# Loading the residual's row tiles one by one between the first stores of a two-layer hybrid encoder

## The chip, the cores and the metric

The kernel runs on one core of a Trainium2 chip. The metric is the device time of one execution in microseconds (us), the median over runs. The core's engines are TensorE (PE in the profile, its weight loads PEld), VectorE (DVE), ScalarE (ACT), GpSimd (POOL) and SyncE (SP), which here issues all transfers. Sixteen DMA engines move the data.

## The reference, cut to what matters

Two encoder layers on 1024 tokens of 1024 channels, in float32. Layer 0 mixes tokens by attention, layer 1 by pooling; each then attends into 256 memory tokens and applies a gated MLP. Before each of these parts stands an RMS norm with a factor (gain) per channel, behind it the residual is added.

```python
def rmsnorm(x, gain):
    x32 = x.astype(jnp.float32)
    y = x32 * lax.rsqrt(jnp.mean(x32 * x32, axis=-1, keepdims=True) + EPS)
    return (y * gain.astype(jnp.float32)).astype(x.dtype)

for i in range(DEPTH):
    if i % N_MIXERS == 0:
        x = x + axial_gqa_attention(rmsnorm(x, attn_norm[ia]), attn_w_qkv[ia],
                                    attn_q_gain[ia], attn_k_gain[ia], attn_w_o[ia])
    ...
    x = x + memory_cross_attention(rmsnorm(x, xattn_norm[i]), rmsnorm(mem, mem_norm[i]),
                                   xattn_w_q[i], xattn_w_kv[i], xattn_w_o[i])
    x = x + conv_gated_ffn(rmsnorm(x, ffn_norm[i]), ffn_w_up[i], ffn_conv_w[i],
                           ffn_conv_b[i], ffn_w_down[i])
return rmsnorm(x, final_norm)
```

The change lies where layer 0's attention ends: `o @ w_o`, the residual, and the norm ahead of the cross-attention.

## The kernel before, in words

The tokens stand in eight row tiles X0 to X7 of 128 tokens x 1024 channels in SBUF, 512 KB each. A product is made as three products of split operands (a high and a low part; lines 746 to 748), accumulated in a PSUM bank. The large products of the cross-attention's query projection are made with seven block products where eight would be usual (class `Seven`): for this the normalised tiles are transposed on TensorE (`turn`, L323) and halves of them are added and subtracted.

`Kernel.run` is the program. `attention` gives the head outputs OT. `load_rows` loads one half (512 columns) of `attn_w_o` in four pieces of 512 KB into the staging buffers `scr` (six of them, shared by all stages) and splits them. Then run loads the tiles X0 to X7 of the input x (L2128) in the order 0, 2, second half of the weights, 4, 6, 1, 3, 5, 7. `cross` follows; its first act is to load the channel factors `xattn_norm` into an `scr` buffer, one copy for each of the 128 partitions (`bcast`, L712, 512 KB), and to make `Seven` with them.

`rows_by` gives three functions for one product of a row tile t with a half n of the weights: `gemm` (24 matmuls into one bank), `add` (the bank onto X[t], L1556), `freed` (gives buffers back). `Seven.begin` runs them in an order written out by hand, 16 steps (n, t): (0,0) (0,2) (1,0) (1,2) (0,4) (1,4) (0,6) (1,6) (0,1) (1,1) (0,3) (1,3) (0,5) (0,7) (1,5) (1,7). Each step does in this order: `gemm`; `free` (here `freed`); at seven of the steps a `turn` of a tile that is done, the first (tile 0) in step (1,2); `add`; `save`, a 256 KB store of the half X[t] to the DRAM tensor Xq (L314), which is read back later as the residual; and, with both halves there, the tile's sum of squares on ScalarE (L727), the root on GpSimd (L719, L721) and `norm` (L318), which overwrites the tile with its normalised values on VectorE. So `norm` needs the factors, the root, and both stores of that tile landed.

All transfers are issued by SP in program order; where SP has to wait for one, all behind it wait. Their completion is counted on eight counters, DMAHW0 to DMAHW7, that are used in turn; a transfer whose counter still has one under way is held until that one, eight places ahead, has landed.

Of the kernel before, what the change touches and what calls it, by code (L numbers as in the profile page):

```python
# [16 lines left out]
P = 128  # L17
# [280 lines left out]
class Seven:  # L298
# [71 lines left out]
    def load(self, f, j):  # L370

        c = self.columns(f)[j]
        src = self.w[:, c:c + P].rearrange("(k p) n -> p k n", p=P)
        self.nc.sync.dma_start(out=self.raws[f][j].rearrange("p (k n) -> p k n", k=NK), in_=src)
# [254 lines left out]
class Kernel:  # L629
# [590 lines left out]

        return (self.R.hv(h).rearrange("p (k n) -> p k n", k=4)[:, k % 4, cols] for h in hs[k // 4 * 2:k // 4 * 2 + 2])

    def cross(self, i, X, steps=None, mixer=None, over={}):

        nc, R, a = self.nc, self.R, self.a
        Xd = self.tc.dram_tile([S, D], F32, name=f"Xq{i}")
        U = Seven(self, a["xattn_w_q"][i], lambda f: (2 * f * P, (2 * f + 1) * P), X, Xd, self.bcast(a["xattn_norm"][i]))
        plan_sums = self.down_sums(i)  # L1230
        q, nf, mem, kT, v, sm, PT, O, wo = {}, D // (2 * P), {}, [], [], {}, {}, {}, {}
        both = lambda t: [(f"X{t}", j) for j in range(2)]
# [6 lines left out]
        def plan_split(plan, name, f, late):  # L1239
# [3 lines left out]
            def high():  # L1243
                hs = q[c] = R.get_halves(1)
                nc.scalar.activation(R.hv(hs[0]), U.bank[f][name], AF.Copy, scale=XHD ** -0.5)

            def low():
                h, l = (R.hv(x) for x in q[c])
                nc.vector.scalar_tensor_tensor(l, U.bank[f].pop(name), XHD ** -0.5, h.bitcast(F32), op0=OP.mult, op1=OP.subtract)
            ins = [(u, 0), (u, 1)]  # L1250
# [184 lines left out]
        def main():  # L1435
            order = U.order(nf)
            if steps:
                U.begin(*steps, lambda: None)
                U.H["T4"] = [R.get(), R.get()]
                over.update({"DVE": 6.5, "ACT": 4.9})  # L1440
            plan = Plan(R, over, {"scr": 2 if steps else 6, "A": 2, "B": 4, "half": len(R.freed)})
            if mixer:
                mixer(plan, U, X)
                order[:4] = [(2, 0), 3, (1, 0), 5, (2, 1), None]
# [673 lines left out]
    def run(self):  # L2118
        nc, R, a = self.nc, self.R, self.a
        OT = self.attention()  # L2120
        ws = [self.load_rows(a["attn_w_o"][0], 0)]
        xp = self.ctx.enter_context(self.tc.tile_pool(name="xres", bufs=1, reuse_waits="tile"))
        X = [xp.tile([P, D], F32, name=f"X{t}") for t in range(NT)]
        for t in (0, 2, None, 4, 6, 1, 3, 5, 7):
            if t is None:
                ws.append(self.load_rows(a["attn_w_o"][0], 1))
            else:
                nc.sync.dma_start(out=X[t], in_=a["x"][0][t * P:(t + 1) * P, :])  # L2128

        def lhs(t, k):  # L2130
            return (R.v(s, 8)[:, k, t % 4 // 2 * P:(t % 4 // 2 + 1) * P] for s in OT[t // 4 * 2 + t % 2])

        def free(t):
            if t % 4 >= 2:
                R.put(*OT[t // 4 * 2 + t % 2])

        steps = self.rows_by(lhs, X, free, lambda n, k: self.blk(ws[n], k, slice(0, 512)), lambda n: R.put(*ws[n]))
        lhs, *ops = self.cross(0, X, steps)
        ready = []
        gemm, add, over = self.ffn(0, lhs, X, *ops, lambda plan: ready.extend([self.pool_weights(plan)]))  # L2140
        lhs, *ops = self.cross(1, X, None, partial(self.pool_mixer, gemm, add, ready[0]), over)
        self.ffn(1, lhs, X, *ops, out=self.out[0])


# [30 lines left out]
```

## Time and profile before

| | us |
|---|---|
| median of 3 runs | 2509.69 (2505.69 to 2514.07) |
| the profiled execution | 2508.51 |
| its span, first to last instruction | 2506.7 |
| TensorE busy in it | 2473.4 |
| VectorE busy in it | 1958.6 |
| ScalarE busy in it | 1348.4 |
| GpSimd busy in it | 436.2 |

The profile shows that one execution; all times within it are microseconds from the start of the span. A row of a timeline has start, length, engine, line, operation, output<-inputs and shapes, and in brackets the idle time ahead of it with what ended it. A row of waits names the waiting engine and line, what it waited for, the total, the number of times and the longest. The granted TensorE clock was 0.998 of full speed over the span. The stage of this change stands between 528 and 634 us.

### The profile page before, as it was taken

How to read it: one execution, taken by the hardware profiler on the slowest of the kernel's cores; microseconds unless marked ns; L12 is line 12 of the kernel's file. 1: busy time of each engine (PE TensorE's matmuls, PEld its weight loads, DVE VectorE, ACT ScalarE, POOL GpSimd, SP SyncE). 2: the span in 40 equal slices, each digit the busy share in tenths (PEclk: the TensorE clock that was granted, in tenths of full speed). 3: DMA queues.
4: the chain of work that ended last, by engine and by line, in shares of the span. 5: the costliest groups of instructions: out<-in, count | busy, mean ns of one | idle time of the engine just before them, and what ended most of it. 6: DMA issues, size and time to landing. Idle time of an engine off the chain costs nothing.

```text
span 2506.7 us, 37225 instructions
## 1 busy us (share of the span) xinstructions
PE 2473.4 (99%) x13435; PEld 2129.7 (85%) x13435; DVE 1958.6 (78%) x2899; ACT 1348.4 (54%) x2307; POOL 436.2 (17%) x594
## 2 busy tenths in 40 slices
PE   9999999999999999999999999999999999999998
PEld 8999999978898888888888888889888888887887
DVE  7779989864986379888889776987559888888875
ACT  6558888852655255555555334655335555554542
POOL 5756666631011000000000003102010000000001
PEclk9999999999999999999999999999999999999999
DMA  7100000042595124243258553388223324337852
GB/s 253 43 2 14 13 14 13 13 171 68 187 317 183 57 79 126 84 122 110 85 170 285 198 182 111 126 283 306 73 72 109 114 84 124 108 93 255 278 189 97
DMA packets 314733, 326.50 MB, mean 130 GB/s; under 512 B 14133, under 2 KB 248861, under 8 KB 314549
## 3 DMA queue, kind: packets, MB, share of 16 engines
q1 hardware_dynamic: 314549, 324.12, 39.9%
q8 instruction: 106, 1.74, 0.3%
q14 instruction: 78, 0.64, 0.1%
HBM read 232.48 MB, written 82.58 MB: 126 GB/s over the span
## 4 chain that ended last, share of the span: by engine, by line
PE 87%; issue 4%; DVE 3%; DMA 2%; ACT 2%; POOL 1%; SPq 0%; POOLq 0%; DVEq 0%; ACTq 0%
PE pB L746 21%; PE pB L748 21%; PE pB L747 21%; PE pA L779 4%; PE pB L740 4%; PE pA L748 3%; PE pA L746 3%; PE pA L747 3%; PE pB L1193 2%; PE pB L1192 2%; DVE R L668 1%; PE pB L323 1%; ACT R L665 1%; DMA scr<-in_ffn_w_down 1%; PE pA L2058 1%
## 5 line engine op out<-in xcount | busy, mean ns | idle before, releaser
L746 PE MATMUL pB<-R,R 128*128 128x512 f32 (+1 forms) x2764 | 1024.3, 371 | 8.4 <-DVE scr L439 3.3
L748 PE MATMUL pB<-R,R 128*128 128x512 f32 (+1 forms) x2760 | 1016.4, 368 | 1.3 <-DVE R L668 1.2
L747 PE MATMUL pB<-R,R 128*128 128x512 f32 (+1 forms) x2764 | 1017.3, 368 | 0.0
L746 PEld LDWEIGHTS pB<-R,R 128*128 128x128 f32 x2764 | 521.1, 189 | 100.7 <-DVE scr L439 4.6
L748 PEld LDWEIGHTS pB<-R,R 128*128 128x128 f32 x2760 | 520.1, 188 | 89.0 <-DVE R L668 2.6
L747 PEld LDWEIGHTS pB<-R,R 128*128 128x128 f32 x2764 | 521.2, 189 | 85.6 <-DVE R L674 0.4
L665 ACT ACTIVATE R<-scr 128x512 fp32r<-128x512 f32 (+2 forms) x340 | 256.9, 781 | 218.3 <-DMA scr<-Gs 60.3
L668 DVE TENSOR_TENSOR R<-scr,R 128x512 fp32r<-128x512 f32 (+2 forms) x340 | 291.6, 887 | 21.5 <-ACT R L665 20.9
L668 DVE TENSOR_TENSOR R<-X,R 128x512 fp32r<-128x512 f32 x374 | 252.5, 686 | 67.5 <-ACT R L665 66.6
L665 ACT ACTIVATE R<-X 128x512 fp32r<-128x512 f32 x374 | 231.7, 630 | 135.8 <-PE pB L747 65.4
L719 POOL TENSOR_SCALAR ms<-ss 128x1 f32<-128x1 f32 (+1 forms) x53 | 14.9, 281 | 1659.0 <-ACT R L727 1280.7
L437 ACT COPY scr<-pB 128x512 f32<-128x512 f32 x156 | 91.3, 585 | 188.3 <-PE pB L748 182.5
L673 ACT ACTIVATE PT<-pB 128x512 fp32r<-128x512 f32 x256 | 140.1, 604 | 56.0 <-PE pB L740 55.7
L789 DVE TENSOR_REDUCE nm<-pA 128x1 f32<-128x1024 f32 x125 | 152.5, 1220 | 20.5 <-PE pA L779 20.5
L674 DVE TENSOR_TENSOR PT<-pB,PT 128x512 fp32r<-128x512 f32 x256 | 163.5, 679 | 5.0 <-ACT PT L673 4.9
L1765 DVE TENSOR_TENSOR X<-pB,X 128x512 f32<-128x512 f32 (+1 forms) x145 | 99.3, 686 | 85.5 <-PE pB L748 84.5
L795 POOL TENSOR_SCALAR scr<-scr,inv 128x1024 f32<-128x1024 f32 x125 | 140.7, 1127 | 70.1 <-DVE inv L794 69.8
L746 PE MATMUL pA<-R,R 128*128 128x512 f32 (+1 forms) x420 | 150.6, 359 | 0.0
L748 PE MATMUL pA<-R,R 128*128 128x512 f32 (+1 forms) x420 | 150.2, 358 | 0.2 <-DVE R L668 0.2
L747 PE MATMUL pA<-R,R 128*128 128x512 f32 (+1 forms) x420 | 150.0, 357 | 0.0
L779 PE MATMUL pA<-R,R 128*128 128x512 f32 x512 | 145.4, 405 | 0.0
L792 ACT ACTIVATE scr<-pA,nm 128x1024 f32<-128x1024 f32 x125 | 139.8, 1118 | 1.5 <-DVE nm L789 0.5
(172 smaller groups left out, 3485.0 us busy)
## 6 DMA issues: line engine op xcount, KB each, us to landing
X<-in_ffn_w_up SPq DMA_DIRECT2D x82, 512.0 KB
Gs<-X SPq DMA_DIRECT2D x105, 256.0 KB
scr<-in_ffn_w_down SPq DMA_DIRECT2D x45, 512.0 KB
scr<-Gs SPq DMA_DIRECT2D x35, 512.0 KB
scr<-in_xattn_w_kv SPq DMA_DIRECT2D x32, 512.0 KB
scr<-Gs SPq DMA_DIRECT2D x42, 384.0 KB
Wt<-scr SPq DMA_DIRECT2D x44, 256.0 KB
Gs<-scr SPq DMA_DIRECT2D x42, 256.0 KB
```

Of the source, the lines that this page charges most:

```text
L665: self.nc.scalar.activation(hi, src, AF.Copy)
L668: self.nc.vector.tensor_tensor(out=lo, in0=src, in1=hi.bitcast(F32), op=OP.subtract)
L673: nc.scalar.activation(hi, src, AF.Copy)
L674: nc.vector.tensor_tensor(out=lo, in0=src, in1=hi.bitcast(F32), op=OP.subtract)
L740: self.nc.tensor.transpose(p[:, k, :], src[:, b * P:(b + 1) * P], self.ident)
L746: mm(out, ah, bh, start=start, stop=False)
L747: mm(out, ah, bl, start=False, stop=False)
L748: mm(out, al, bh, start=False, stop=stop)
L779: nc.tensor.matmul(s[:, kh * 512:(kh + 1) * 512], q, R.v(K[part][kh], 4)[:, kv], start=part == 0, stop=part == 1)
L789: nc.vector.tensor_reduce(nm, s, axis=AX.X, op=OP.max, negate=True)
L792: nc.scalar.activation(pr, s, AF.Exp, bias=nm, accum_out=rs)
L795: nc.gpsimd.tensor_scalar(pr, pr, ri, 1.0, op0=OP.mult, op1=OP.mult)
```

## The change

`run` loads only tiles 0, 2 and 4 ahead of the residual, and the channel factors between the weights' second half and tile 4. The tiles 6, 1, 3, 5 and 7 are loaded one by one from a function `between` that takes the place of `freed` in the steps: in step (1,2) tile 6, in (0,4) tile 1, in (1,4) tile 3, in (1,6) tile 5, in (0,1) tile 7. `between` runs ahead of its step's `add` and `save`, so on SP's queue each load stands directly behind the store of the step before. `cross` gets the factors as an argument; for layer 1 they are loaded at the call, which is the same place on the queue.

```diff
-    def cross(self, i, X, steps=None, mixer=None, over={}):
+    def cross(self, i, X, gain, steps=None, mixer=None, over={}):
...
-        U = Seven(self, a["xattn_w_q"][i], lambda f: (2 * f * P, (2 * f + 1) * P), X, Xd, self.bcast(a["xattn_norm"][i]))
+        U = Seven(self, a["xattn_w_q"][i], lambda f: (2 * f * P, (2 * f + 1) * P), X, Xd, gain)
...
-        for t in (0, 2, None, 4, 6, 1, 3, 5, 7):
-            if t is None:
-                ws.append(self.load_rows(a["attn_w_o"][0], 1))
-            else:
-                nc.sync.dma_start(out=X[t], in_=a["x"][0][t * P:(t + 1) * P, :])
+
+        def load(t):
+            nc.sync.dma_start(out=X[t], in_=a["x"][0][t * P:(t + 1) * P, :])
+        load(0)
+        load(2)
+        ws.append(self.load_rows(a["attn_w_o"][0], 1))
+        gain = self.bcast(a["xattn_norm"][0])
+        load(4)
+        later = {(1, 2): 6, (0, 4): 1, (1, 4): 3, (1, 6): 5, (0, 1): 7}
...
-        steps = self.rows_by(lhs, X, free, lambda n, k: self.blk(ws[n], k, slice(0, 512)), lambda n: R.put(*ws[n]))
-        lhs, *ops = self.cross(0, X, steps)
+        gemm, add, freed = self.rows_by(lhs, X, free, lambda n, k: self.blk(ws[n], k, slice(0, 512)), lambda n: R.put(*ws[n]))
+
+        def between(n, t):
+            freed(n, t)
+            if (n, t) in later:
+                load(later[n, t])
+        steps = gemm, add, between
+        lhs, *ops = self.cross(0, X, gain, steps)
...
-        lhs, *ops = self.cross(1, X, None, partial(self.pool_mixer, gemm, add, ready[0]), over)
+        lhs, *ops = self.cross(1, X, self.bcast(a["xattn_norm"][1]), None, partial(self.pool_mixer, gemm, add, ready[0]), over)
```

SP's queue from behind the weights' second half on, before: X0_ to X7_ are the row tiles, scr_ is the buffer of the factors, Xq0_ the tensor that the stores write; in brackets what SP waits for.

```order
L2128 DMA X4_7408<-in_x 128x1024 [waits DMAHW1_49,PE_49]
L2128 DMA X6_7410<-in_x 128x1024 [waits DMAHW2_49,PE_49]
L2128 DMA X1_7405<-in_x 128x1024 [waits DMAHW3_49]
L2128 DMA X3_7407<-in_x 128x1024 [waits DMAHW4_49]
L2128 DMA X5_7409<-in_x 128x1024 [waits DMAHW5_49]
L2128 DMA X7_7411<-in_x 128x1024 [waits DMAHW6_49]
L712 DMA scr_7439<-in_xattn_norm 128x1024 [waits DMAHW7_49,Pool_49]
L314 DMA Xq0_7438<-X0_7404 128x512 [waits DMAHW0_49,DVE_49]
L314 DMA Xq0_7438<-X2_7406 128x512 [waits DMAHW1_49,DVE_49]
L314 DMA Xq0_7438<-X0_7404 128x512 [waits DMAHW2_49,DVE_49]
L314 DMA Xq0_7438<-X2_7406 128x512 [waits DMAHW3_49,DVE_49]
```

The same place of the changed kernel:

```order
L712 DMA scr_7430<-in_xattn_norm 128x1024 [waits DMAHW2_49,DMAHW1_49,Pool_49]
L2126 DMA X4_7408<-in_x 128x1024 [waits PE_49]
L314 DMA Xq0_7435<-X0_7404 128x512 [waits DMAHW5_49,DMAHW3_49,DVE_49]
L314 DMA Xq0_7435<-X2_7406 128x512 [waits DMAHW6_49,DMAHW4_49,DVE_49]
L314 DMA Xq0_7435<-X0_7404 128x512 [waits DVE_49]
L2126 DMA X6_7410<-in_x 128x1024 [waits PE_49]
L314 DMA Xq0_7435<-X2_7406 128x512 [waits DMAHW7_49,DVE_49]
L2126 DMA X1_7405<-in_x 128x1024 [waits DMAHW0_49]
L314 DMA Xq0_7435<-X4_7408 128x512 [waits DMAHW2_49,DMAHW1_49,DVE_49]
L2126 DMA X3_7407<-in_x 128x1024
```

Five loads have gone from ahead of tile 0's second store, the third of the stores, to places behind it, and the factors stand ahead of tile 4.

VectorE at the first two norms, before:

```order
L1556 TENSOR_TENSOR X0_7404<-pB_7507,X0_7404 128x512 [waits PE_49]
L318 SCALAR_TENSOR_TENSOR X0_7404<-X0_7404,rs_7539,scr_7439 128x1024 [waits DMAHW2_49,DMAHW0_49,DMAHW7_49,Activation_49,Pool_49]
L1556 TENSOR_TENSOR X2_7406<-pB_7542,X2_7406 128x512 [waits PE_49]
L318 SCALAR_TENSOR_TENSOR X2_7406<-X2_7406,rs_7584,scr_7439 128x1024 [waits DMAHW1_49,DMAHW3_49,Activation_49,Pool_49]
L674 TENSOR_TENSOR R3_70<-pB_7567,R2_69 128x4x128 [waits PE_49,Activation_49]
L674 TENSOR_TENSOR R5_72<-pB_7568,R4_71 128x4x128 [waits PE_49,Activation_49]
L1556 TENSOR_TENSOR X4_7408<-pB_7593,X4_7408 128x512 [waits PE_49]
```

And of the changed kernel:

```order
L1556 TENSOR_TENSOR X0_7404<-pB_7502,X0_7404 128x512 [waits PE_49]
L318 SCALAR_TENSOR_TENSOR X0_7404<-X0_7404,rs_7534,scr_7430 128x1024 [waits DMAHW3_49,DMAHW1_49,DMAHW5_49,Activation_49,Pool_49]
L1556 TENSOR_TENSOR X2_7406<-pB_7537,X2_7406 128x512 [waits PE_49]
L318 SCALAR_TENSOR_TENSOR X2_7406<-X2_7406,rs_7580,scr_7430 128x1024 [waits DMAHW4_49,DMAHW7_49,Activation_49,Pool_49]
L674 TENSOR_TENSOR R3_70<-pB_7563,R2_69 128x4x128 [waits PE_49,Activation_49]
L674 TENSOR_TENSOR R5_72<-pB_7564,R4_71 128x4x128 [waits PE_49,Activation_49]
L1556 TENSOR_TENSOR X4_7408<-pB_7589,X4_7408 128x512 [waits DMAHW2_49,PE_49]
```

No instruction of VectorE has moved. The norm waits for the same transfers under other counters (the factors and the tile's two stores), and the first add of tile 4, as those of tiles 6, 1, 3, 5 and 7, now waits for its load by a counter of its own. TensorE, ScalarE and GpSimd issue the same instructions in the same order.

## Prediction

> **What bounds the kernel now.** I read the page first (busy shares and the chain), then TensorE's waits over the whole run, then the chain, the stretches and the timelines around the one long wait.
>
> ```profile
> span 2506.7 us, 37225 instructions
> ...
> PE 2473.4 (99%) x13435; PEld 2129.7 (85%) x13435; DVE 1958.6 (78%) x2899; ACT 1348.4 (54%) x2307; POOL 436.2 (17%) x594
> ...
> PE 87%; issue 4%; DVE 3%; DMA 2%; ACT 2%; POOL 1%; SPq 0%; POOLq 0%; DVEq 0%; ACTq 0%
> ```
>
> TensorE is busy 99% of the span, and the chain that ends last runs over it. A change that moves only transfers can win only where TensorE now stands still. Its waits, longest in total first (us, times, longest):
>
> ```profile
> PE pB L323 <- DVE X L318: 3.9, 2, 3.5
> PE pB L746 <- DVE scr L439: 3.3, 6, 1.0
> PE pB L740 <- POOL scr L795: 3.0, 5, 1.0
> ```
>
> The longest single one, 3.5 us, is a transpose (L323, `turn`) waiting for the normalisation of a row tile (L318, `norm`). The others are at most 1.0 us each, at places that the change doesn't touch. The chain through the long one (start, length, what):
>
> ```profile
> 545.75 0.70 DVE X L1556
> ...
> 546.47 6.66 DMA Xq<-X
> ...
> 553.35 1.29 DVE X L318
> ...
> 554.69 1.09 PE pB L323 x8
> ```
>
> This is step (1,0) of the residual: the second half of tile 0 is added (L1556) and stored (Xq<-X), and `norm` may overwrite the tile only when the store has landed, 6.66 us after its issue. VectorE's waits in the stretch 515 to 660 us show what is usual:
>
> ```profile
> DVE X L318 <- POOL rs L721: 13.6, 6, 2.6
> DVE X L318 <- DMA Xq<-X: 6.9, 1, 6.9
> ```
>
> Six norms waited at most 2.6 us, for GpSimd's root (L721), and one waited 6.9 us, for the store. Why that store is slow is told by the stretches (last two columns: share of the DMA engines' time, GB/s) and by SP's queue:
>
> ```profile
> 540.00:546.00 6.00, 6.00 (x29) 4.95 (x27) 3.40 (x4) 2.12 (x2) 0.00 (x0) 1.00 1.03 419
> 546.00:551.00 5.00, 5.00 (x23) 3.94 (x21) 0.44 (x1) 1.15 (x2) 0.75 (x2) 1.00 0.97 375
> 551.00:555.00 4.00, 0.46 (x4) 0.32 (x4) 1.65 (x2) 0.00 (x0) 0.00 (x0) 1.00 0.05 19
> 555.00:561.00 6.00, 6.00 (x32) 5.05 (x30) 2.72 (x4) 3.10 (x6) 0.76 (x2) 1.00 0.11 44
> ```
> ```profile
> 533.51 5.56 SPq L2128 DMA_DIRECT2D X<-in_x  x6
> 540.07 0.33 SPq L712 DMA_DIRECT2D scr<-in_xattn_norm  x1
> ...
> 542.86 0.33 SPq L314 DMA_DIRECT2D Xq<-X  x1
> ...
> SPq L314 <- DMA X<-in_x: 1.9, 2, 1.0
> ```
>
> Until 551 the DMA engines are full, then almost idle: the store was issued behind six tile loads and the factors. SP's last row times the loads: a transfer waits for the one eight places ahead (the counters in the order's rows above), so the store at 542.86 went out when tile 4 had landed (about 542.8, after 1.0 us of waiting), and the next store waited the other 0.9 us, from about 543.2 to 544.1, for tile 6. That is 1.25 us for a 512 KB load in a full queue (419 GB/s).
>
> **The change part by part.** It adds and removes no instruction of TensorE, VectorE, ScalarE or GpSimd. SP issues the same eight loads, one factor row and stores in another order.
>
> *Five loads leave the queue ahead of the store.* Before, from the landing of tile 6 at 544.1: four tiles and the factors, 5 x 1.25 = 6.25 us, two stores of half the size, 2 x 0.63, and the store itself, 0.63, give 552.2 by this count. The stretches have the engines full to 551 and the chain has the landing at 553.13 (546.47 + 6.66), so 1 to 2 us lie between the last byte and the signal. Now only the factors and tile 4 follow the last weight piece:
>
> ```profile
> 541.42 1.06 ACT L673 ACTIVATE R<-scr 128x1024 fp32r<-128x1024 f32 x1 [0.33 <-DMA scr<-in_attn_w_o]
> ...
> 533.68 0.75 POOL L1206 TENSOR_TENSOR R<-scr,R 128x256 fp32r<-128x256 f32 x1
> ```
>
> The piece has landed at 541.4; plus 2 x 1.25 and two stores, 2 x 0.63, that is 545.2. The store issued at 546.47 finds an empty queue. The factors now wait for GpSimd's L1206, whose buffer they take, until 534.43, and tile 4 behind them leaves about 1 us later than now; both still stand behind that piece, so this costs nothing.
>
> *How fast a store lands in an empty queue* bounds the rest:
>
> ```profile
> 568.38 0.32 SPq L314 DMA_DIRECT2D Xq<-X  x1
> ...
> 570.54 1.28 DVE L318 SCALAR_TENSOR_TENSOR X<-X,rs,scr 128x1024 f32<-128x1024 f32 x1 [2.19 <-POOL rs L721]
> ...
> 878.37 0.69 DVE L1556 TENSOR_TENSOR X<-pB,X 128x512 f32<-128x512 f32 x1 [1.27 <-PE pB L748]
> 882.04 1.28 DVE L318 SCALAR_TENSOR_TENSOR X<-X,rs,scr 128x1024 f32<-128x1024 f32 x1 [2.97 <-DMA Xd<-X]
> ```
>
> At most 2.2 us in the first case (570.54 - 568.38; the norm waited for GpSimd), and 3.0 us in the second, where the store itself was waited for (from the add's end, 879.06, to 882.04). So the first norm starts between 548.7 and 549.4; the lower end is also where its root is ready:
>
> ```profile
> 548.04 0.56 POOL L721 TENSOR_TENSOR rs<-ms,mh 128x1 f32<-128x1 f32 x1
> ```
>
> The norm takes 1.28 us: done between 550.0 and 550.7. TensorE's rows say when it is wanted, and what the stall costs:
>
> ```profile
> 550.76 0.39 PE L748 MATMUL pB<-R,R 128*128 128x512 f32 x1
> 554.69 1.09 PE L323 MATMUL pB<-ident,X 128*128 128x128 f32 x8 [3.54 <-DVE X L318]
> 555.54 0.48 PE L746 MATMUL pB<-R,R 128*128 128x512 f32 x1
> ...
> 560.89 0.39 PE L748 MATMUL pB<-R,R 128*128 128x512 f32 x1
> 561.12 1.03 PE L323 MATMUL pB<-ident,X 128*128 128x128 f32 x8
> 561.91 0.48 PE L746 MATMUL pB<-R,R 128*128 128x512 f32 x1
> ```
>
> Unstalled, a transpose starts 0.23 us after the last matmul (561.12 - 560.89). So this one could start at 550.99, and the norm is done by then at either end. It started 3.93 us after: the stall is 3.93 - 0.23 = 3.70 us, and it goes whole. I take **-3.7 us**; its lower end is below, among the rivals.
>
> *Loads that now follow a store at once.* Tile 6 is issued behind the first norm's last store, tile 1 behind the second's, tile 7 behind the fourth's. If store and load were served together, the store would land with the load: 0.63 + 1.25 of moving and 2.2 - 0.63 = 1.5 around it, 3.4 us. The first norm would then end 546.47 + 3.4 + 1.28 = 551.15, 0.2 us late; a later one has 3.2 us to land (572.90 - 1.28 - 568.38 less some 0.05 for the signal, by the transpose below, which the norm of 570.54 serves), so 0.2 each. The ends are 0 and 0.6 in all; served in order it is 0, which the first store's own place in the queue speaks for. I take 0.
>
> ```profile
> 572.90 0.93 PE L323 MATMUL pB<-ident,X 128*128 128x128 f32 x7
> ```
>
> *Loads that come later.* The additions now wait for their tiles' loads. Tile 6 has the least time: issued behind the store of 546.47, first used by the add that stands at 573.10 before and at 569.4 with the stall gone.
>
> ```profile
> 573.10 0.69 DVE L1556 TENSOR_TENSOR X<-pB,X 128x512 f32<-128x512 f32 x1 [1.27 <-PE pB L748]
> ...
> 531.12 0.93 SPq L2128 DMA_DIRECT2D X<-in_x  x2
> ...
> 538.75 0.33 SPq L2128 DMA_DIRECT2D X<-in_x  x1
> ```
>
> That leaves 22 us. The slowest load of before, tile 2's, went out by 531.7 and had landed when tile 7's issue, which waits for it, ran at 538.75: 7 us, in a full queue. So this costs 0. On SP itself a load is 0.3 to 0.6 us of issue, with over 4 us to the next store: 0.
>
> *The second layer's factors* are loaded at the same place as before (the call moved, the queue didn't): 0.
>
> *Does the win reach the end?* What follows waits for engines, and nearly all of TensorE's other waits are on VectorE, ScalarE or GpSimd, which move with it. Sum: 2506.7 - 3.7 = 2503.0 of span; with the profiled execution's 1.8 outside the span, 2504.8. That execution (2508.51) is 1.2 below the median of the three runs, 2509.69, so the median becomes **2506.0 us**, -0.15%. That is less than the 0.3% that a measurement of this kernel can tell from no change: its three runs alone span 0.33%.
>
> **The rivals.**
> *The stall is only shortened.* The store to memory lands in more than 3.2 us (550.99 - 1.28 - 546.47, less 0.05), for the load behind it or for the two stores ahead. For: no row shows a store with a load issued right behind it and a norm waiting for it. Against: 3.0 us at the worst seen. Half of the stall left gives 2507.9.
> *The store is slow for another reason than the queue,* and nothing goes: 2509.7. Against it: only this one of the norms in the stage waits for its store, and the DMA engines are full to within 2 us of its landing.
> *Slower: loads are late at the additions.* Five adds each wait for a tile, and TensorE soon waits behind them. Fully exposed, a load costs 1.25 us (full queue) to 7 us (tile 2's): 5 x 1.25 - 3.7 = +2.6, 2512.3; 5 x 7 - 3.7 = +31, 2541. It decides only where a load takes over 22 us, which nothing here comes near. [...]
> *The stall also slowed the matmuls after it,* by a lower clock, and more is won. Had the clock been halved for as long as the stall, 1.8 us would come on top: 2504.2. Against: the granted clock is 1.00 in the stretches 551 to 555 and 555 to 561 above, and the first and last matmul after the stall lie 5.35 us apart (555.54 to 560.89), 24 of them at 0.23. [...]
>
> **How the numbers follow.** The stall goes whole: 0.80. Shortened: 0.10. Nothing goes: 0.05. Late loads: 0.02. Clock, or a gain elsewhere that I don't see: 0.03. The first three lie within 0.3% by themselves; the runs' spread (-0.16% to +0.17% about the median) carries some 0.05 of them past -0.3% and 0.01 past +0.3%. So faster 0.07, same 0.90, slower 0.03. The range is the runs of before, 2505.7 to 2514.1, moved by -3.7, which is 2502.0 to 2510.4; it takes in the shortened stall and the case of no change.
>
> **What would show it.** Right: in the changed kernel's trace the norm of tile 0 waits for L721 like the others; the wait of L323 on L318 falls from 3.9 to about 0.4; the store at (1,0) lands within 3 us; the DMA engines are full until about 545 and then carry some 130 GB/s until 577 (the 44 of before and 2.6 MB in 30 us); no L1556 waits for X<-in_x. Wrong: L318 still waits for Xq<-X, an add waits for X<-in_x, or TensorE's waits after 560 grow by what was won.

## The result, and the profile after

The changed kernel takes 2504.18 us, median of 9 runs (2502.41 to 2506.69), beside 2511.61 us for the kernel before in its 9 (2505.69 to 2514.21). The ratio is 0.9977, 95% interval 0.9968 to 0.9985: a gain of 3.8 to 8.0 us, by its middle 5.8 (the two medians alone lie 7.4 apart). The interval leaves out 1, so there is a gain; by its middle it is smaller than the 0.3% that the prediction counted as the least change to be told from none. The profiled execution took 2504.04 us.

The page's span and chain by engine:

```profile
span 2502.3 us, 37230 instructions
...
PE 88%; issue 4%; DVE 3%; ACT 2%; POOL 1%; DMA 1%; POOLq 0%; ACTq 0%; DVEq 0%; SPq 0%
```

TensorE's waits over the run, the longest and the one in question:

```profile
PE pB L740 <- POOL scr L795: 4.5, 5, 1.2
...
PE pB L323 <- DVE X L318: 0.4, 1, 0.4
```

The wait of 3.5 us is gone; what is left of the row is the 0.4 of another place, which was there before. TensorE at the first two transposes:

```profile
551.72 0.39 PE L748 MATMUL pB<-R,R 128*128 128x512 f32 x1
551.95 1.03 PE L323 MATMUL pB<-ident,X 128*128 128x128 f32 x8
...
558.30 1.03 PE L323 MATMUL pB<-ident,X 128*128 128x128 f32 x8
```

The transpose of tile 0 starts 0.23 us behind the last matmul, as an unstalled one does. VectorE's rows of the first two norms, and SP's at the first moved load:

```profile
546.71 0.69 DVE L1556 TENSOR_TENSOR X<-pB,X 128x512 f32<-128x512 f32 x1 [1.89 <-PE pB L748]
550.20 1.28 DVE L318 SCALAR_TENSOR_TENSOR X<-X,rs,scr 128x1024 f32<-128x1024 f32 x1 [2.80 <-DMA Xq<-X]
...
567.71 1.28 DVE L318 SCALAR_TENSOR_TENSOR X<-X,rs,scr 128x1024 f32<-128x1024 f32 x1 [2.18 <-POOL rs L721]
...
579.92 1.29 DVE L318 SCALAR_TENSOR_TENSOR X<-X,rs,scr 128x1024 f32<-128x1024 f32 x1 [2.60 <-DMA Xq<-X]
```
```profile
547.43 0.32 SPq L314 DMA_DIRECT2D Xq<-X  x1
547.80 1.21 SPq L2126 DMA_DIRECT2D X<-in_x  x1
```

The store went out at 547.43 and the norm started at 550.20, 2.8 us later instead of 6.9. The norm ends at 551.48, 0.47 us before the transpose starts. The first norm still waits for its store and not for the root. Behind 556 us TensorE's waits did not grow by what was won: the largest row there, L746 on L439, is 2.2 us in total, beside 3.3 before.

From the start of the second add of tile 0, (1,0), to the transpose of tile 2 it was 561.12 - 545.75 = 15.37 us in the profile before and is 558.30 - 546.71 = 11.59 us now: 3.78 less. This stretch is the measure of the experiments below, since a whole execution varies by several microseconds and this place, unstalled, does not: from the one transpose to the next it is 6.33 to 6.42 us in all five profiles without a stall.

### The profile page after: what moved, and what is told of

Same layout as the page of the kernel before. It is cut to its first block, busy times and chain, and to the rows that moved or that the text cites. A ratio compares the mean times of both kernels' runs of the same rounds, so it can differ in the third digit from the quotient of the medians.

```text
span 2502.3 us, 37230 instructions
## 1 busy us (share of the span) xinstructions
PE 2471.6 (99%) x13435; PEld 2128.4 (85%) x13435; DVE 1958.8 (78%) x2899; ACT 1347.4 (54%) x2307; POOL 434.9 (17%) x594
## 4 chain that ended last, share of the span: by engine, by line
PE 88%; issue 4%; DVE 3%; ACT 2%; POOL 1%; DMA 1%; POOLq 0%; ACTq 0%; DVEq 0%; SPq 0%
PE pB L746 21%; PE pB L748 21%; PE pB L747 21%; PE pA L779 5%; PE pB L740 4%; PE pA L748 3%; PE pA L746 3%; PE pA L747 3%; PE pB L1193 2%; PE pB L1192 2%; DVE R L668 1%; PE pB L323 1%; ACT R L665 1%; DMA X<-in_ffn_w_up 1%; PE pA L2058 1%
## 5 line engine op out<-in xcount | busy, mean ns | idle before, releaser
L746 PE MATMUL pB<-R,R 128*128 128x512 f32 (+1 forms) x2764 | 1024.1, 371 | 7.1 <-DVE scr L439 2.2
L746 PEld LDWEIGHTS pB<-R,R 128*128 128x128 f32 x2764 | 520.8, 188 | 99.2 <-DVE R L668 3.4
L746 PE MATMUL pA<-R,R 128*128 128x512 f32 (+1 forms) x420 | 150.6, 359 | 0.0
```

The costliest lines, as they stand in the source:

```text
L746: mm(out, ah, bh, start=start, stop=False)
```

## The experiments

Three theories stood against each other. The queue: tile 0's store is late because tile loads stand ahead of it. The factors: what helps is that they load earlier. The clock: standing still also slows the matmuls behind it. The runs e1 to e4 have 11 executions each, beside 33 of the kernel before (median 2510.24 us); e5 to e12 have one each, so for these only the profile counts. The edits of e2 to e7 are shown against the changed kernel, those of e8 and e9 against the kernel before.

**The kernel before against itself (e1).** No edit.

> The kernel before, unchanged, against itself: what the comparison calls no change, and how often the granted clock falls after the stall. Theory of the queue (the store of tile 0's second half stands behind five tile loads and the factors): ratio 1.000 within 0.15%, the store lands again 6.5 to 6.9 us after its issue, TensorE waits 3.5 us at L323, and the stretch behind it runs at clock 1.00. Rival, the clock: in some executions the 3.5 us of standing still lower the clock for the matmuls behind it, so that the stall costs up to 1.8 us more than its length; then this profile or its runs show a lower clock than the changed kernel's.

Ratio 1.0001 (0.9992 to 1.0010). The wait at L323 was 3.5 us, the stretch 560.04 - 544.68 = 15.36 us, the clock 1.00 behind the stall. So the same kernel, measured twice, agrees within 0.1%.

**The loads alone (e2).**

```diff
-        gain = self.bcast(a["xattn_norm"][0])
-        load(4)
+        load(4)
+        gain = self.bcast(a["xattn_norm"][0])
```

> The five loads moved, but the factors loaded behind tile 4 as before. Queue theory: the bytes ahead of the store are the same as in the changed kernel, so the store lands within 3 us, TensorE doesn't wait at L323 for tile 0, and the time is that of the changed kernel, -3.7 us or more against before (ratio 0.9970 to 0.9990). Rival, the factors: if it is their place that helps, the norm of tile 0 waits for them and a stall of 1 us or more comes back.

Ratio 0.9982 (0.9973 to 0.9991), 2505.01 us. TensorE did not wait for the norm:

```profile
551.01 0.39 PE L748 MATMUL pB<-R,R 128*128 128x512 f32 x1
551.24 1.03 PE L323 MATMUL pB<-ident,X 128*128 128x128 f32 x8
...
557.57 1.03 PE L323 MATMUL pB<-ident,X 128*128 128x128 f32 x8
```

The stretch was 557.57 - 545.99 = 11.58 us, that of the changed kernel. The loads alone bring the gain.

**The factors alone (e3).**

```diff
-        load(4)
-        later = {(1, 2): 6, (0, 4): 1, (1, 4): 3, (1, 6): 5, (0, 1): 7}
+        for t in (4, 6, 1, 3, 5, 7):
+            load(t)
+        later = {}
```

> Only the factors moved ahead of tile 4; all eight tiles are loaded up front. Queue theory: the same bytes stand ahead of the store as before, so it lands again some 6.7 us after issue, TensorE waits 3.5 us at L323, and the time is that of before (ratio 0.9985 to 1.0015). Rival, the factors: the stall goes, -3.7 us.

Ratio 1.0003 (0.9994 to 1.0011). The store landed 6.5 us after its issue, and the stall was there again:

```profile
549.16 0.39 PE L748 MATMUL pB<-R,R 128*128 128x512 f32 x1
552.82 1.09 PE L323 MATMUL pB<-ident,X 128*128 128x128 f32 x8 [3.28 <-DVE X L318]
...
560.85 1.03 PE L323 MATMUL pB<-ident,X 128*128 128x128 f32 x8
```

The theory of the factors falls. These rows hold something else: 8.03 us lie between the two transposes (560.85 - 552.82), and 6.43 in the profile before (561.12 - 554.69). The kernel lost 1.6 us *behind* its stall, at a granted clock of 0.50 (third column from the right):

```profile
555.00:557.00 2.00, 2.00 (x7) 1.54 (x6) 1.44 (x2) 1.55 (x4) 0.53 (x1) 0.50 0.00 0
```

**Each load in the step that adds its tile (e4).**

```diff
-        later = {(1, 2): 6, (0, 4): 1, (1, 4): 3, (1, 6): 5, (0, 1): 7}
+        later = {(0, t): t for t in (6, 1, 3, 5, 7)}
```

> The changed kernel with each of the five loads moved as late as it can stand: into the very step that adds the tile. Queue theory: the load stands behind the store of the step before and so goes out as the step's matmuls begin, some 5.4 us ahead of the add; it lands in about 3 us (1.25 of moving and 1.5 around it), so no add waits for X<-in_x by more than 0.5 us and TensorE for none: the time of the changed kernel within 0.1%. Rival, late loads: each of five adds waits 1.25 to 7 us and TensorE with them, +6 to +35 us against the changed kernel.

Ratio 0.9980 (0.9971 to 0.9989), 2505.13 us, beside the 0.9977 of the change; stretch 558.49 - 546.83 = 11.66 us. No add waited for a load. The reason stands in SP's queue and VectorE's rows:

```profile
566.16 0.38 SPq L2126 DMA_DIRECT2D X<-in_x  x1
```
```profile
568.37 1.28 DVE L318 SCALAR_TENSOR_TENSOR X<-X,rs,scr 128x1024 f32<-128x1024 f32 x1 [2.65 <-DMA Xq<-X]
570.47 0.69 DVE L1556 TENSOR_TENSOR X<-pB,X 128x512 f32<-128x512 f32 x1 [0.82 <-PE pB L748]
```

Tile 6 goes out at 566.16, behind the store of the step before, and its add, at 570.47, waits for TensorE. So even the latest place on the queue leaves this load 4.3 us, where 5.4 were forecast. Late loads are not in reach of this schedule.

**One, two and three loads moved, and two more put ahead (e5 to e8).** The kernel before with part of the change, the factors in their old place behind the loads; the fourth loads tiles 1 and 3 a second time behind tile 7.

```diff
+        for t in (4, 6, 1, 3, 5):       # e5; e6: (4, 6, 1, 3); e7: (4, 6, 1)
+            load(t)
         gain = self.bcast(a["xattn_norm"][0])
-        load(4)
-        later = {(1, 2): 6, (0, 4): 1, (1, 4): 3, (1, 6): 5, (0, 1): 7}
+        later = {(0, 1): 7}             # e6: and (1, 6): 5; e7: and (1, 4): 3
...
-        for t in (0, 2, None, 4, 6, 1, 3, 5, 7):
+        for t in (0, 2, None, 4, 6, 1, 3, 5, 7, 1, 3):     # e8
```

> The kernel before with only the last tile load (7) moved behind the first stores; the factors behind the other loads. Queue theory: 1.25 us less stands ahead of the store, so it lands 5.4 us after issue and TensorE's wait at L323 is 3.5 - 1.25 = 2.3 us. Rival (the store is slow for another reason): 3.5 us as before.

> Tiles 5 and 7 moved. Queue theory: the store lands 4.2 us after issue, wait at L323 3.5 - 2.5 = 1.0 us. Rival: 3.5 us.

> Tiles 3, 5 and 7 moved. Queue theory: the store lands 2.9 us after issue, inside the 3.2 us that it has, so the wait at L323 is 0 to 0.2 us: three of the five loads are enough. Rival: 3.5 us, or a rest that only the fourth and fifth take away.

> The kernel before with tiles 1 and 3 loaded a second time behind tile 7 (the same bytes into the same place), so 1 MB more stands ahead of the store. Queue theory: the store lands 6.7 + 2.5 = 9.2 us after issue or later (a second load of a tile also holds SP until the first has landed), and TensorE's wait at L323 is 3.5 + 2.5 = 6.0 us or more. Rival: 3.5 us. The clock: if standing still lowers it, it shows in the stretch behind a stall of 6 us.

The norm's wait on VectorE in e5, e6, e7 and e8, in this order:

```profile
551.94 1.28 DVE L318 SCALAR_TENSOR_TENSOR X<-X,rs,scr 128x1024 f32<-128x1024 f32 x1 [5.25 <-DMA Xq<-X]
```
```profile
551.20 1.29 DVE L318 SCALAR_TENSOR_TENSOR X<-X,rs,scr 128x1024 f32<-128x1024 f32 x1 [3.48 <-DMA Xq<-X]
```
```profile
551.17 1.28 DVE L318 SCALAR_TENSOR_TENSOR X<-X,rs,scr 128x1024 f32<-128x1024 f32 x1 [3.00 <-DMA Xq<-X]
```
```profile
554.79 1.28 DVE L318 SCALAR_TENSOR_TENSOR X<-X,rs,scr 128x1024 f32<-128x1024 f32 x1 [8.68 <-DMA Xq<-X]
```

| loads moved | -2 (added) | 0 | 1 | 2 | 3 | 5 |
|---|---|---|---|---|---|---|
| norm's wait for its store, us | 8.68 | 6.91 | 5.25 | 3.48 | 3.00 | 2.80 (after), 3.10 (e2), 3.20 (e4) |
| TensorE's wait at L323, us | 5.3 | 3.5 | 1.9 | 0.3 | none | none |

Each of the first two loads takes 1.7 us off the wait (I had forecast 1.25), the third 0.5, the other two nothing that can be told: the wait levels out near 3 us, what a store takes there with little ahead of it. Two of the five are almost enough, three are enough, by one profile each. The two added loads bring 1.8 us instead of 2.5, and there the store also went out late: SP, held up by the second loads, issued it at 547.10, 1.0 us after its add had ended (546.10), and it landed 7.57 us after that, where 9.2 or more were forecast. The sizes are rough, since in the five profiles of the kernel before (the last three are below) the same wait is 6.89 to 7.75 us. From two loads added to two moved it falls by 5.20 us, or 1.30 a load.

**The store on another queue (e9).** The kernel before, with that one store issued by ScalarE; this moves the lines by 3.

```diff
-        self.nc.sync.dma_start(out=self.Xd[t * P:(t + 1) * P, c], in_=self.X[t][:, c])
+        e = self.nc.scalar if (n, t) == (1, 0) and not getattr(self.kn, "stored", False) else self.nc.sync
+        if e is self.nc.scalar:
+            self.kn.stored = True
+        e.dma_start(out=self.Xd[t * P:(t + 1) * P, c], in_=self.X[t][:, c])
```

> The kernel before, all loads up front, but the one store of tile 0's second half is issued by ScalarE on its own DMA queue instead of SP's. If the store is late because it stands behind the loads on SP's queue (order within a queue), it now is served beside them and lands in 2 to 4 us, and TensorE's wait at L323 falls from 3.5 to at most 0.5 us with nothing else moved. If it is late because the DMA engines are full whatever the queue, it lands again 6 us or more after issue and the wait stays at 3 us or more.

ScalarE issued it at 546.83. The norm waited 6.67 us and TensorE 3.3, as with SP:

```profile
546.83 0.34 ACTq L317 DMA_DIRECT2D Xq<-X  x1
```
```profile
553.47 1.28 DVE L321 SCALAR_TENSOR_TENSOR X<-X,rs,scr 128x1024 f32<-128x1024 f32 x1 [6.67 <-DMA Xq<-X]
```

The DMA queues (q1 is SP's, q10 ScalarE's) in the stretches 546.83 to 549.5 and 549.5 to 553.5, with packets, MB and share of the 16 engines:

```profile
q1 hardware_dynamic: 324, 1.00, 95.2%
```
```profile
q1 hardware_dynamic: 202, 0.36, 24.2%
q10 hardware_dynamic: 144, 0.26, 17.0%
```

For 2.7 us behind its issue the store moved no packet, while SP's queue kept the engines busy (95.2%). Up to 550.0, 3.2 us behind the issue, there was still none; from 550.0 to 550.5 there were 42, as SP's share fell to 53%. A store with nothing ahead of it (kernel before, issued at 568.38) has its first packets 0.7 to 0.9 us behind the issue, so at least 2.3 us of the 3.2 are delay. So another queue did not take it past the loads. The wait alone would not show this, since the norm also needs tile 0's first store and the factors, which stayed on SP's queue; the packets do. Why the second queue was not served beside the first stays open.

**Three more profiles of the kernel before (e10, e11, e12).** No edit.

> The kernel before, one more look at the stretch behind the stall. Clock theory (new): standing still for 3.5 us halves the granted clock in some executions, by where it falls; then about every second look shows 0.50 in the stretch behind it and 17 us instead of 15.4 from the add of (1,0) to the transpose of tile 2. Rival: the kernel before always keeps 1.00, as in the two looks so far, and it is the other order of the loads that lost the clock.

> As the look ahead of it: 15.4 us at clock 1.00, or 17 us with 0.50 behind the stall.

> As the two looks ahead of it: 15.4 us at clock 1.00, or 17 us with 0.50 behind the stall.

All three show the lower clock, 0.50 at its lowest in each. The first, with TensorE's rows and the stretches (third column from the right: granted clock):

```profile
549.18 0.39 PE L748 MATMUL pB<-R,R 128*128 128x512 f32 x1
553.94 1.97 PE L323 MATMUL pB<-ident,X 128*128 128x128 f32 x8 [4.38 <-DVE X L318]
...
563.17 1.03 PE L323 MATMUL pB<-ident,X 128*128 128x128 f32 x8
```
```profile
551.00:553.00 2.00, 0.00 (x0) 0.00 (x0) 0.40 (x1) 0.00 (x0) 0.00 (x0) 1.00 0.03 12
553.00:555.00 2.00, 1.06 (x5) 1.06 (x6) 1.49 (x2) 0.43 (x1) 0.00 (x0) 0.52 0.00 0
555.00:557.00 2.00, 2.00 (x9) 1.71 (x8) 0.32 (x1) 2.00 (x5) 0.75 (x2) 0.50 0.34 131
557.00:559.00 2.00, 2.00 (x6) 1.62 (x5) 2.00 (x3) 0.66 (x2) 0.00 (x0) 0.50 0.00 0
559.00:561.00 2.00, 2.00 (x8) 1.56 (x8) 0.17 (x1) 0.00 (x0) 0.00 (x0) 0.77 0.00 0
561.00:563.00 2.00, 2.00 (x11) 1.62 (x10) 0.00 (x0) 0.00 (x0) 0.00 (x0) 1.00 0.00 0
```

From 553 to about 560 the clock is half (0.50), and the eight transposes take 1.97 us instead of 1.03. From transpose to transpose it is 9.23 us (563.17 - 553.94), 2.80 more than the 6.43 at full clock. The same in e5, behind a stall of 1.9 us:

```profile
553.00:555.00 2.00, 1.72 (x10) 1.62 (x11) 0.83 (x2) 1.09 (x3) 0.00 (x0) 0.74 0.15 58
555.00:557.00 2.00, 2.00 (x6) 1.52 (x5) 0.96 (x1) 2.00 (x5) 0.76 (x2) 0.50 0.19 73
557.00:559.00 2.00, 2.00 (x9) 1.64 (x8) 1.52 (x3) 0.01 (x1) 0.00 (x0) 0.90 0.00 0
```

The five profiles of the kernel before; the stall is the gap between the starts of the last matmul and the transpose less 0.23 us, the loss behind it the time from transpose to transpose less 6.43:

| profile | before | e1 | e10 | e11 | e12 | mean |
|---|---|---|---|---|---|---|
| stall, us | 3.70 | 3.68 | 4.53 | 3.86 | 4.00 | 3.95 |
| lost behind it at the lower clock, us | 0 | 0 | 2.80 | 2.46 | 1.58 | 1.37 |

By the same count e3 lost 1.60 us, e5 1.60, e8 2.14 and e9 1.33. So of nine profiles with a wait of 1.9 us or more here, seven show the lower clock behind it (e3, e5, e8 to e12) and two do not (before, e1); of the five without (after, e2, e4, e6, e7) none does at this place. e9 to e12 ran on one chip and e1 to e4 on another; on the latter e1 kept its clock and e3 did not, so it is not a matter of the one chip.

Nor does it take this stall. In the profile before itself the clock had been 0.50 from about 525.6 to 529, ahead of the stall:

```profile
528.00:534.00 6.00, 6.00 (x27) 4.82 (x27) 3.25 (x3) 2.40 (x3) 2.31 (x3) 0.91 0.57 191
```

TensorE had waited three times there within some 3 us, for 0.97, 0.31 and 0.34 us. In e4 this place lost the clock too, with waits of 0.9, 0.3 and 0.3 us (0.98 over 500 to 528, 0.94 over 528 to 551); in the changed kernel it had the same waits (1.00, 0.31, 0.34) and kept 1.00 from 524 to 530. In e6 and e7, with 0.3 us of stall and none, the clock is 1.00 from 500 to 565, and yet its mean over the span is 0.998, so it fell elsewhere.

How often it happens in executions without a profile can be estimated from each run's mean granted clock, which is on record to three digits. It is 0.99811 over the 44 runs of the kernel before that belong to e1 to e4, and 0.99859 over the 22 of e2 and e4; 0.00048 of 2507 us is 1.2 us. The 44 runs take 2510.07 us in the mean and the 22 take 2505.13, 4.9 less. Among those with a clock of 0.999 it is 2508.50 (18 runs) and 2504.35 (14), 4.2 less, near the stall's own length.

## Why the prediction was right or wrong

**The place and the cause: right.** The store was late by the transfers ahead of it (e5 to e8: the wait follows their number), the loads are what counts (e2), the factors' place brings nothing that the runs show (e3), and the stall went whole. In the profile the stretch is 3.78 us shorter, with 3.7 forecast.

**The store's landing: right in the changed kernel, by a thin margin.** Between 2.2 and 3.0 us were forecast, about 2.8 measured; but in e2 and e4, with the same five loads moved, the norm waited 3.10 and 3.20. In e4 it ends at 552.00 (550.72 + 1.28), 0.07 us ahead of its transpose at 552.07. That the stall went whole every time was in part luck. The norm was said to wait for the root like the others; it still waits for the store, which the prediction lists as a sign of being wrong, but inside the 3.2 us that it has, so TensorE doesn't. The 1 to 2 us read as lying between the last byte and the signal are mostly a thin rest of packets: from 551 to 552.75 the profile before shows 45 of them, 0.08 MB, and the store landed at 553.13. The price of a load in the full queue, 1.25 us, is not refuted by e5 to e8: 1.7 for each of the first two, 1.30 over four. With five loads moved this changed nothing.

**A load directly behind a store: right, hidden.** The norm of tile 6 (last store followed at once by a load) now waits 2.60 us for the store, that of tile 4 (none follows) 2.18 us for the root. In e4 a load follows tile 4's last store instead, and its norm, at 568.37 in the row above, waits 2.65 us for the store. It costs at least some 0.4 us (a root that comes last hides when the store landed) and stays inside the time there is. I took 0 for the path, and it was 0.

**Late loads: right.** No add waits for a load, not even in e4. At this place the runs show no gain in issuing earlier than e4 does: tile 6 issued 22 us ahead of its add (570.28 - 547.80, the changed kernel) or 4 us ahead (e4) gives the same time within the intervals (0.9977 and 0.9980), and the loads issued at once held up a store, for which the norm waited 6.9 us instead of 2.8.

**The clock: wrong.** The prediction gave 0.03 to "clock, or a gain elsewhere" and put the loss behind the stall at nothing in its sum. The step that failed is the argument against that rival: the clock of 1.00 behind the stall was read from one profiled execution and taken for the kernel. In three of the kernel's other four profiles the clock did fall there. The term that was put at nothing is 1.4 us as a mean of five profiles, and 1.2 by the mean clock of the runs, both estimates. With the stall's mean of 3.95 the five profiles make 5.3 us, beside 5.8 (3.8 to 8.0) measured for the change and 4.5 and 5.0 for e2 and e4 (their ratios times 2510). The 1.8 us that the prediction put on this rival, half the clock for as long as the stall, were its estimate. As a rule the runs don't show that: by it e5 would have lost 1.0 us and e10 2.3 (half of 2.04 and 4.53, the stalls by the count of the table), and they lost 1.60 and 2.80; over the seven profiles it was 1.3 to 2.8 us. Nor does the stall's length alone tell whether the clock falls: it fell behind 1.9 us (e5) and stayed at 1.00 behind 3.70 and 3.68 (before, e1). What decides it, no run shows.

**The time: right in sign and range,** 2506.0 forecast in 2502.0 to 2510.4 against 2504.18. The range takes in no change as well, so it decides little. The kernel before itself went from 2509.69 in the median of 3 runs to 2511.61 in that of 9, so the absolute time came out nearer than the gain did. The gain of 3.7 us lies just outside the near end of the interval (3.8 to 8.0); the clock's term fits the missing part.

## What to carry to other kernels

Before loads are queued up front, look for a small store behind them on which the next step waits. Here each of the first two loads of 512 KB that left the queue ahead of it took 1.7 us off the wait and the third 0.5, to 3.0 us; only so many need to move as bring the store inside the time that it has, three of the five. A pause of TensorE may cost more than its length, by the clock behind it: 1.3 to 2.8 us more in seven profiles of nine here. One profile doesn't tell whether it does, so compare the stretch behind the pause over several executions.

## What the runs showed of the hardware that was not expected

- The granted clock fell to 0.50 behind pauses of TensorE of 1.9 to 5.3 us in seven profiles of nine, and cost 1.3 to 2.8 us each (the least in e9, the most in e10). Pauses of 3.5 us left it at 1.00 in the other two. Three waits of 0.3 to 1.0 us within some 3 us were followed by 0.50 in the profile before (525.6 to 529), by a lower clock in e4's (0.94 over 528 to 551) and by 1.00 in the changed kernel's (524 to 530).
- A store issued on ScalarE's queue moved no packet for 2.7 us while SP's queue kept the DMA engines 95% busy; with nothing ahead of it, a store has its first packets within 0.9 us (kernel before, issued at 568.38).
